# A given order of products for the merging projections of a two-branch encoder layer, with source tiles loaded one at a time

## The chip, the cores and the metric

The kernel runs on one core of a Trainium2 chip. The core has five engines with a queue of instructions each: TensorE (PE, matrix products, with its weight loads shown apart as PEld), VectorE (DVE), ScalarE (ACT), GpSimd (POOL) and SyncE (SP, which here only issues DMAs). Each engine runs its own queue in order, and semaphores make it wait for the others. DMAs are issued from the queues of SP, ACT and POOL. Operands lie in an on-chip memory of 128 partitions (SBUF); matrix products are summed up in banks of 128 x 512 numbers (PSUM). The metric is the device time of one execution in microseconds (us); of several runs the median counts.

## What is computed

One encoder layer is applied to two groups of 512 tokens with the same weights, in float32. What matters here is the middle of the layer, where two branches are projected to the model's width, merged by gates, and projected once more:

```python
y_m = (jax.nn.sigmoid(o) * hm.astype(x.dtype)) @ w_mo      # branch (A), mLSTM
...
y_a = mla_attention(q_nope, q_rope, k_nope, k_rope, va) @ w_ao   # branch (B), attention
g_m, g_a = jnp.split(jax.nn.sigmoid(gm), 2, axis=-1)
x = x + (g_m * y_m + g_a * y_a) @ w_out
```

Both `w_mo` and `w_ao` are 1024 x 1024. The feed-forward network, a gated embedding and a last norm follow.

## The kernel before, in words

**Exact products out of rounded ones.** PE multiplies a rounded float32 type. Each operand is therefore cut into a rounded part (hi: a cast on ACT) and the rest (lo: a subtraction on DVE, `lo_of`, L168), and each product is made of three matmuls: hi x hi, hi x lo, lo x hi. In `product` these are the lines L857, L858 and L859; for four slices of 128 rows a product has 12 matmuls of 128 x 512.

**Seven products in place of eight.** The class `Seven` multiplies a pair of column blocks (c and c + 4) of a weight with both token groups at once. With two blocks of weights and two groups there would be eight half-length products; it makes seven, named P1, P2, P7, P6, P5, Q4 and P3, from sums of the weight's four quarters a11, a12 (the first source tile of 512 KB) and a21, a22 (the second). `source` makes these sums in place: for P7 s = a11 + a21 (L818) and a21 += a22 (L819), for P6 a11 += a21 (L821), for P3 a12 += a11 (L828). They run on POOL, but for three pairs on DVE (the first and the last of `w_mo`, the first of `w_ao`). The other factor's sums and cuts are made by `Ops.part` and `Ops.need` (L748 to L770). The products of a pair are summed up in three banks: b1 takes P1, then P6, P5 and P3, and between them ACT copies it (L911); b0 takes P2; b2 takes P7, then Q4. DVE combines them (L916), and `put_z` or `put_y` multiplies with the gate and adds (L1239, L1520, L1521).

**The stage.** There are eight pairs: 0 to 3 for `w_mo` (operands `hops`), 4 to 7 for `w_ao` (operands `oops`, the attention's output). P1, P2, P7 and P6 of pair 0 run inside the last units of the attention, whose instructions keep an order written out by hand (`pinned`). In the loop over units, u is the unit, and the slots named "a", "mid", "d", "late" and so on hold extra work for it; `pairs[i].ahead` cuts a weight early there. The 52 other products run in `chain(quads, made=pairs, ...)` (the call follows L1530). Its order before, with the pair's number ahead of the product's name:

```
1P1 1P2 1P7 0P5 0Q4 0P3 | 1P6 2P1 1P5 2P2 1Q4 2P7 1P3 | 2P6 3P1 2P5 3P2 2Q4 3P7 2P3
3P6 4P1 3P5 4P2 3Q4 4P7 3P3 | 4P6 5P1 4P5 5P2 4Q4 5P7 4P3 | 5P6 6P1 5P5 6P2 5Q4 5P3
6P6 6P7 6P5 7P1 6Q4 6P3 | 7P6 7P7 7P5 7P2 7Q4 7P3
```

This is the order in which the instructions are traced. A planner with a simulated timeline then orders each engine's queue from it, and it may move instructions past each other, unless they are told to keep the program's order (`pinned`, or for matmuls `mmpin`) or to be issued behind another instruction of the same engine (`issue_after`).

**Buffers.** Cut weights have five buffers in turn (`wpair`), hi and lo of a product side by side, so a weight can be cut when the product five before it has been done. Source tiles: `wring` gives a pair's first tile one of three buffers in turn (two in pool WP, one in OP), the second tile one of two (pool WX). A pair's first tile is read until P3's cut, its second until Q4's. Both are loaded in the constructor of `Seven` (`S.dma_start`, L804), that is from ACT's queue, when `chain` makes the pair, one product ahead of its first use. The operands P1, P2, P7 and P6 lie in 32 buffers of pool H, and those of `oops` take over those of `hops`; P5, Q4 and P3 lie in 24 buffers of pool OP. `chain` asks for operands four products ahead (`look`).

**After the stage.** The merged values are cut (L1541, L1543) and go into `out_proj` (L197 to L199); later the feed-forward network runs through `chain` again, with `head=True`.

Of the kernel before, what the change touches and what calls it, by code (L numbers as in the profile page):

```python
# [62 lines left out]
def encoder_kernel(ctx: ExitStack, tc: tile.TileContext, a):  # L63
# [3 lines left out]
    class Engine:  # L67


        def __init__(self, e):  # L70
            self.e = e
# [133 lines left out]
    def rsqrt(src, n, scale):  # L205
# [22 lines left out]
        return y2  # L228

# [545 lines left out]
    wpn, wsn = [0], [0]  # L775
# [12 lines left out]
    def wsplit(src):  # L788
        n, t = src.shape[-1], wpair()
        hi, lo = t[:, 0:n], t[:, n : 2 * n]  # L790
        S.copy(hi, src)  # L791
        lo_of(lo, src, hi)
        return hi, lo

    class Seven:


        def __init__(self, srcs, kh, ops, out, adds=None):
            n = kh * P
            self.adds = adds or GP  # L800
            st = []
            for sl, src in zip(wring(wsn[0]), srcs):
                t = sl("wst", "wst", F32, (P, 1024))
                S.dma_start(t[:, : 2 * n], src)  # L804
                st += [t[:, 0:n], t[:, n : 2 * n]]
            wsn[0] += 1
            self.st, self.n, self.kh, self.ops, self.out = st, n, kh, ops, out
            self.bk, self.w = {}, {}

        def source(self, name):  # L810
            n, (a11, a12, a21, a22) = self.n, self.st
# [18 lines left out]
            return src  # L830

# [31 lines left out]
    def chain(quads, head=False, look=4, made=(), done=(), two=False, hook=None):  # L863

        order = [(0, n) for n in ("P1", "P2", "P7")]
# [22 lines left out]
        order = [o for o in order if o not in done]  # L888
# [5 lines left out]
        for at, (q, n) in enumerate(order):  # L894
            for i, m in order[at : at + look + 1]:
                quads[i][0].need(m)
            for i, _ in order[at : at + 2]:
                make(i)
            mmpin[0] = head and q == len(quads) - 1
            made[q].product(n)  # L900
            mmpin[0] = False
            if hook and (q, n) in hook:
                hook[q, n]()
# [340 lines left out]
    def pair(kind, c, ops, put):  # L1244
        e = V if (kind, c) in (("mo", 0), ("mo", 3), ("ao", 0)) else GP
        srcs = [a["w8"][W8[f"{kind}{i}"]] for i in (c, c + 4)]
        return ops, lambda: Seven(srcs, 4, ops, outputs(put), e)
# [55 lines left out]
    for u in range(NU + 1):  # L1303
# [83 lines left out]
        if u == 14:  # L1387
            todo_ = {"mid": [(ahead_hi, "P2")], "d": [(ahead_lo, "P2")], "late": [(ahead_hi, "P7")], "f": [(ahead_lo, "P7")]}
        pre = lambda name, out=True: pairs[0].product(name, out)
# [138 lines left out]
    with ExitStack() as behind:  # L1528
# [4 lines left out]
        chain(quads, made=pairs, done=[(0, n) for n in ("P1", "P2", "P7", "P6")])  # L1533
# [205 lines left out]
    chain(quads, head=True)  # L1739
# [162 lines left out]

LEAD = 2
# [98 lines left out]
```

## Time and profile before

| | us |
|---|---|
| three timed runs | 1850.92, 1852.28, 1853.04 |
| their median | 1852.28 |
| the profiled execution | 1848.15 |
| its span, from the first to the last instruction | 1846.4 |

The profile is of one execution. It gives the busy time of each engine and a chain of work that ended last. A row of the timeline has a start in us from the span's start, a length in us, the engine, the line of the kernel (L79 stands for all instructions with a pinned order), the operation, the tiles as out<-in, shapes, and in brackets the engine's idle time before it with what ended that. Matmuls are pipelined: each is shown with its full length of about 0.39 us, though the next starts earlier, so the time from start to start says more than the length. ACTq, SPq are the queues' issuing of DMAs, which does not count as busy. The granted clock of PE was 0.997 of full speed over the span.

### The profile page before, as it was taken

What the parts mean: (1) busy time and instruction counts of PE and PEld (TensorE: products, weight loads), DVE (VectorE), ACT (ScalarE), POOL (GpSimd) and SP (SyncE); (2) the same over time, 40 slices, a digit from 0 to 9 for tenths busy, and PEclk for the clock granted to TensorE, in tenths of its full rate; (3) what the DMA queues carried; (4) which work ended last, traced back from release to release, by engine and by line L of the source; (5) the groups of instructions that cost most, each with busy time, mean ns of one, the idle gap of its engine ahead of it and who ended that gap; (6) DMA issues with size and microseconds to landing.
All of it is one profiled execution on the core that took longest, in us unless ns stands there. A gap on an engine that the chain in (4) does not pass through costs nothing.

```text
span 1846.4 us, 24616 instructions
## 1 busy us (share of the span) xinstructions
PE 1817.5 (98%) x8767; PEld 1512.0 (82%) x8767; DVE 1281.5 (69%) x2154; ACT 892.1 (48%) x1752; POOL 429.8 (23%) x353
## 2 busy tenths in 40 slices
PE   9999999999999999999999999999999999999997
PEld 7889898988887888877877888888888887888786
DVE  6767576857667787778887586444444569978756
ACT  6256556563454566664543364333333344434433
POOL 0101010200032222213420005664566523111000
PEclk9999999999999999999999999999999999999998
DMA  4211112123353443267555331322223246533332
GB/s 168 67 58 52 63 52 71 45 75 126 126 172 128 149 137 115 81 211 239 183 177 185 113 141 69 126 92 97 97 91 131 97 157 237 161 133 100 103 141 99
DMA packets 104619, 224.65 MB, mean 122 GB/s; under 512 B 12856, under 2 KB 23536, under 8 KB 104496
## 3 DMA queue, kind: packets, MB, share of 16 engines
q1 hardware_dynamic: 85440, 158.02, 25.6%
q10 hardware_dynamic: 13248, 47.19, 7.6%
q0 software_dynamic: 5808, 17.86, 3.0%
q8 instruction: 69, 1.13, 0.3%
q14 instruction: 54, 0.44, 0.1%
HBM read 164.57 MB, written 54.26 MB: 119 GB/s over the span
## 4 chain that ended last, share of the span: by engine, by line
PE 85%; DVE 9%; ACT 2%; DMA 2%; issue 1%; POOL 0%; SPq 0%; DVEq 0%; ACTq 0%
PE b L857 13%; PE b L859 13%; PE b L858 12%; PE mm L197 6%; PE mm L199 6%; PE mm L198 6%; PE sc L79 4%; PE mm L79 3%; PE nm L643 3%; PE l L79 3%; PE av L79 2%; PE pt L79 1%; PE mm L563 1%; DVE xl L168 1%; PE mm L562 1%; PE mm L561 1%
## 5 line engine op out<-in xcount | busy, mean ns | idle before, releaser
L857 PE MATMUL b<-xh,wp 128*128 128x512 f32 x1051 | 403.8, 392 | 7.0 <-ACT wp L791 4.3
L858 PE MATMUL b<-xl,wp 128*128 128x512 f32 x1051 | 409.5, 391 | 0.7 <-DVE xl L168 0.7
L859 PE MATMUL b<-xh,wp 128*128 128x512 f32 x1051 | 406.9, 391 | 2.0 <-DVE wp L168 2.0
L791 ACT CAST wp<-wst 128x512 fp32r<-128x512 f32 (+1 forms) x289 | 176.2, 613 | 304.2 <-PE b L859 247.0
L168 DVE TENSOR_TENSOR wp<-wst,wp 128x512 fp32r<-128x512 f32 (+1 forms) x289 | 246.4, 855 | 73.8 <-ACT wp L791 68.9
L857 PEld LDWEIGHTS b<-xh,wp 128*128 128x128 f32 x1051 | 197.3, 188 | 55.2 <-ACT u L911 6.3
L859 PEld LDWEIGHTS b<-xh,wp 128*128 128x128 f32 x1051 | 197.3, 188 | 45.8 <-DVE wp L168 2.8
L858 PEld LDWEIGHTS b<-xl,wp 128*128 128x128 f32 x1051 | 197.3, 188 | 43.6 <-DVE xl L168 1.1
L197 PE MATMUL mm<-hh,whi 128*128 128x512 f32 x432 | 169.2, 392 | 0.1
L198 PE MATMUL mm<-hl,whi 128*128 128x512 f32 x432 | 168.8, 391 | 0.0
L199 PE MATMUL mm<-hh,wlo 128*128 128x512 f32 x432 | 168.2, 391 | 0.0
L916 DVE TENSOR_TENSOR u<-b,u 128x512 f32<-128x512 f32 x95 | 65.3, 688 | 139.0 <-PE b L859 80.5
L818 POOL TENSOR_TENSOR s<-wst,wst 128x512 f32<-128x512 f32 (+1 forms) x33 | 56.2, 1702 | 333.0 <-DMA wst<-w 163.2
L1661 POOL TENSOR_TENSOR sg<-sg,u 128x512 f32<-128x512 f32 x30 | 55.0, 1833 | 202.6 <-DVE u L916 202.6
L911 ACT COPY u<-b 128x512 f32<-128x512 f32 x93 | 52.6, 588 | 94.9 <-PE b L859 67.6
L199 PEld LDWEIGHTS mm<-hh,wlo 128*128 128x128 f32 x432 | 81.1, 188 | 16.9
L197 PEld LDWEIGHTS mm<-hh,whi 128*128 128x128 f32 x432 | 81.1, 188 | 16.7 <-ACT raw L79 0.5
L198 PEld LDWEIGHTS mm<-hl,whi 128*128 128x128 f32 x432 | 81.1, 188 | 16.6
L182 ACT CAST whi<-wst 128x1024 fp32r<-128x1024 f32 x53 | 55.6, 1049 | 73.9 <-PE mm L198 36.4
L168 DVE TENSOR_TENSOR xl<-ld,xh 128x512 fp32r<-128x512 f32 x105 | 84.3, 830 | 0.6 <-ACT xh L1692 0.5
L609 POOL TENSOR_TENSOR b<-b,mask 128x512 f32<-128x512 f32 x16 | 24.5, 1536 | 228.4 <-DMA b<-nmd 169.4
L168 DVE TENSOR_TENSOR wlo<-wst,whi 128x1024 fp32r<-128x1024 f32 (+2 forms) x56 | 67.1, 1199 | 12.1 <-ACT whi L182 11.7
(446 smaller groups left out, 4034.5 us busy)
## 6 DMA issues: line engine op xcount, KB each, us to landing
wst<-w ACTq DMA_DIRECT2D x68, 512.0 KB
wst<-w SPq DMA_DIRECT2D x65, 512.0 KB
ld<-actd SPq DMA_DIRECT2D x77, 256.0 KB
actd<-t SPq DMA_DIRECT2D x40, 256.0 KB
x<-x SPq DMA_DIRECT2D x32, 256.0 KB
wst<-wd ACTq DMA_DIRECT2D x16, 512.0 KB
actd<-sg SPq DMA_DIRECT2D x30, 256.0 KB
ld<-hzd SPq DMA_DIRECT2D x28, 256.0 KB
```

The lines of the kernel that those rows point to most:

```text
L79: r = f(*args, **kw)
L168: e.tensor_tensor(out=out, in0=src, in1=hi.bitcast(F32), op=ALU.subtract)
L182: S.copy(hi[:, :n], st[:, :n])
L197: E.matmul(bk, whi[:, c], hi, start=k == 0, stop=False)
L198: E.matmul(bk, whi[:, c], lo, start=False, stop=False)
L199: last_mm[0] = E.matmul(bk, wlo[:, c], hi, start=False, stop=k == nk - 1)
L791: S.copy(hi, src)
L818: self.adds.tensor_tensor(out=src, in0=a11, in1=a21, op=ALU.add)
L857: E.matmul(bk, whi[:, c], hi, start=bool(first) and k == 0, stop=False, **sk)
L858: E.matmul(bk, whi[:, c], lo, start=False, stop=False, **sk)
L859: E.matmul(bk, wlo[:, c], hi, start=False, stop=k == self.kh - 1, **sk)
L916: V.tensor_tensor(out=t, in0=b, in1=t, op=ALU.add if name == "P2" else ALU.subtract)
```

## The change

Five things change.

- `chain` can be given an order, and the merging projections get one, `MERGE`. Up to the product 1Q4 it is the order from before; then the pairs 2 and 3 alternate product by product, and after them 4 and 5; 6 and 7 follow as before. The matmuls of pair 7 keep their program order, with 7P2 and 7Q4 between 7P5 and 7P3.
- `Seven` can be made without its loads (`parts=True`, for all pairs but 0 and 1), and `fetch` loads one source tile. In `MERGE`, `2w` behind a product fetches the next tile of pair 2; the load is issued on ACT behind the latest cast of a weight (`cast[0]`).
- The two sums for P7 of pair 1 are made by POOL in the attention's unit 14, the last but one, in slot "a" (`summed`), and `source` later returns the ready tile.
- In the chain of the feed-forward network the loads of the first pairs are issued behind the last weight cast of the merging projections (`after=merged`).
- A tile of 32 bytes a partition, `pad`, is allocated in the pool `sm` and never used.

```diff
+    sm.tile([P, 8], F32, name="pad", tag="pad", bufs=1)
...
-    wpn, wsn = [0], [0]
+    wpn, wsn, cast = [0], [0], [None]
...
-        S.copy(hi, src)
+        cast[0] = S.copy(hi, src).ins
         lo_of(lo, src, hi)
...
-        def __init__(self, srcs, kh, ops, out, adds=None):
+        def __init__(self, srcs, kh, ops, out, adds=None, parts=False):
             n = kh * P
             self.adds = adds or GP
-            st = []
-            for sl, src in zip(wring(wsn[0]), srcs):
-                t = sl("wst", "wst", F32, (P, 1024))
-                S.dma_start(t[:, : 2 * n], src)
-                st += [t[:, 0:n], t[:, n : 2 * n]]
+            self.st, self.n, self.kh, self.ops, self.out = [], n, kh, ops, out
+            self.todo = list(zip(wring(wsn[0]), srcs))
             wsn[0] += 1
-            self.st, self.n, self.kh, self.ops, self.out = st, n, kh, ops, out
-            self.bk, self.w = {}, {}
+            while self.todo and not parts:
+                self.fetch()
+            self.bk, self.w, self.made = {}, {}, {}
+
+        def fetch(self):
+            sl, src = self.todo.pop(0)
+            t = sl("wst", "wst", F32, (P, 1024))
+            S.dma_start(t[:, : 2 * self.n], src)
+            self.st += [t[:, 0 : self.n], t[:, self.n : 2 * self.n]]

         def source(self, name):
-            n, (a11, a12, a21, a22) = self.n, self.st
+            if name in self.made:
+                return self.made[name]
+            n, (a11, a12, a21, a22) = self.n, (self.st + [None] * 2)[:4]
...
+        def summed(self, name, e):
+            e, self.adds = self.adds, e
+            self.made[name] = self.source(name)
+            self.adds = e
...
-    def chain(quads, head=False, look=4, made=(), done=(), two=False, hook=None):
+    def chain(quads, head=False, look=4, made=(), done=(), two=False, hook=None, order=None, after=None):
...
-        order = [o for o in order if o not in done]
+        if given:
+            order = [(int(o[0]), o[1:]) for o in given if o[1] != "w"]
+            fetch = {}
+            for o in given:
+                if o[1] == "w":
+                    fetch.setdefault(at, []).append(int(o[0]))
+                else:
+                    at = int(o[0]), o[1:]
+        else:
+            order = [o for o in order if o not in done]
...
             for i, _ in order[at : at + 2]:
-                make(i)
-            mmpin[0] = head and q == len(quads) - 1
+                with tc.issue_after(after) if after and at < 4 else nullcontext():
+                    make(i)
+            mmpin[0] = (head or given) and q >= len(quads) - (1 if head else 1)
             made[q].product(n)
             mmpin[0] = False
+            for i in fetch.get((q, n), ()) if given else ():
+                with tc.issue_after(cast[0]):
+                    make(i)
+                    made[i].fetch()
...
-        return ops, lambda: Seven(srcs, 4, ops, outputs(put), e)
+        return ops, lambda: Seven(srcs, 4, ops, outputs(put), e, c > 1 or kind == "ao")
...
             todo_ = {"mid": [(ahead_hi, "P2")], "d": [(ahead_lo, "P2")], "late": [(ahead_hi, "P7")], "f": [(ahead_lo, "P7")]}
+            todo_["a"] = todo_.get("a", []) + [(lambda: pairs[1].summed("P7", GP),)]
...
-        chain(quads, made=pairs, done=[(0, n) for n in ("P1", "P2", "P7", "P6")])
+        chain(quads, made=pairs, order=MERGE.split())
+        merged = cast[0]
...
-    chain(quads, head=True)
+    chain(quads, head=True, after=merged)
...
+MERGE = """
+1P1 2w 1P2 1P7 0P5 0Q4 2w 0P3 3w 1P6 2P1 1P5 2P2 1Q4 3P1 3w 1P3 3P2 4w
+2P7 3P7 2P6 3P6 2P5 3P5 2Q4 4P1 4w 2P3 4P2 5w 3Q4 5P1 5w 3P3 5P2 6w
+4P7 5P7 4P6 5P6 4P5 5P5 4Q4 6P1 6w 4P3 6P2 7w 5Q4 5P3 7w
+6P6 6P7 6P5 7P1 6Q4 6P3 7P6 7P7 7P5 7P2 7Q4 7P3
+"""
```

More of the change, by code (lines that the diff above doesn't have):

```diff
@@ L1 @@
-from contextlib import ExitStack
+from contextlib import ExitStack, nullcontext
 import concourse.bass as bass
@@ L861, in product @@
                 self.out(name, self.bk)
-    def chain(quads, head=False, look=4, made=(), done=(), two=False, hook=None):
-        order = [(0, n) for n in ("P1", "P2", "P7")]
+    def chain(quads, head=False, look=4, made=(), done=(), two=False, hook=None, order=None, after=None):
+        given, order = order, [(0, n) for n in ("P1", "P2", "P7")]
         if head:
```

## The prediction

> **What bounds the kernel now.** I read the page first, for the engine that sets the end.
>
> ```profile
> span 1846.4 us, 24616 instructions
> ...
> PE 1817.5 (98%) x8767; PEld 1512.0 (82%) x8767; DVE 1281.5 (69%) x2154; ACT 892.1 (48%) x1752; POOL 429.8 (23%) x353
> ...
> PE 85%; DVE 9%; ACT 2%; DMA 2%; issue 1%; POOL 0%; SPq 0%; DVEq 0%; ACTq 0%
> ```
>
> TensorE is busy for 98% of the span and holds 85% of the chain that ended last. The change removes no matmul, so all that it can give is idle time of PE. I therefore went to the busy time by stretch, for the 52 products that the chain of merging projections still has to run when it starts at 836 us. Columns: stretch, its length, busy us (and count) of PE, weight loads, DVE, ACT, POOL, then granted clock, DMA share, GB/s.
>
> ```profile
> 836.00:852.00 16.00, 12.39 (x53) 9.26 (x51) 14.18 (x18) 11.57 (x23) 12.87 (x7) 1.00 0.71 233
> 852.00:922.00 70.00, 70.00 (x306) 57.37 (x307) 60.98 (x96) 31.19 (x56) 21.96 (x6) 1.00 0.61 200
> 922.00:930.00 8.00, 5.56 (x24) 3.88 (x23) 8.00 (x13) 5.25 (x11) 0.50 (x1) 1.00 0.86 247
> 930.00:950.00 20.00, 20.00 (x89) 16.43 (x88) 19.50 (x26) 6.93 (x13) 6.16 (x4) 1.00 0.61 191
> 950.00:988.00 38.00, 36.65 (x159) 29.51 (x158) 32.70 (x50) 17.65 (x30) 5.81 (x4) 1.00 0.59 198
> 836.00:988.00 152.00, 144.60 (x625) 116.44 (x624) 135.37 (x200) 72.59 (x129) 47.30 (x21) 1.00 0.63 204
> ```
>
> The second row has no idle PE: 70.00 / 306 = 0.2288 us a matmul, so a product of 12 takes 2.745 us. 52 products need 142.8 us; the stage takes 152.0. **The most that this stage can give is 9.2 us**, 0.5% of the kernel. By the rows PE idles 152.00 - 144.60 = 7.40 us; the other 1.8 us are restarts. The timeline shows where (start, length, engine, line, operation, idle time before and what ended it):
>
> ```profile
> 837.98 4.63 POOL L818 TENSOR_TENSOR s<-wst,wst 128x512 f32<-128x512 f32 x1
> 842.64 0.62 ACT L791 CAST wp<-s 128x512 fp32r<-128x512 f32 x1 [3.07 <-POOL s L818]
> 843.31 0.50 PE L857 MATMUL b<-xh,wp 128*128 128x512 f32 x1 [1.25 <-ACT wp L791]
> 844.44 1.78 DVE L168 TENSOR_TENSOR xl<-ld,xh 128x512 fp32r<-128x512 f32 x1
> 849.55 0.68 DVE L916 TENSOR_TENSOR u<-b,u 128x512 f32<-128x512 f32 x1
> 849.68 0.50 PE L858 MATMUL l<-xl,wp 128*128 128x512 f32 x1 [0.80 <-DVE xl L168]
> 851.97 0.50 PE L859 MATMUL b<-xh,wp 128*128 128x512 f32 x1 [1.56 <-DVE wp L168]
> ...
> 903.04 7.04 POOL L818 TENSOR_TENSOR s<-wst,wst 128x512 f32<-128x512 f32 x1 [41.62 <-DMA wst<-w]
> 910.15 8.94 POOL L819 TENSOR_TENSOR wst<-wst 128x512 f32<-128x512 f32 x1
> 919.17 1.63 POOL L821 TENSOR_TENSOR wst<-wst,wst 128x512 f32<-128x512 f32 x1
> 919.57 1.78 DVE L168 TENSOR_TENSOR wp<-wst,wp 128x512 fp32r<-128x512 f32 x1
> 923.68 0.62 ACT L770 CAST xh<-t 128x512 fp32r<-128x512 f32 x1 [3.23 <-DVE t L757]
> 924.21 0.61 ACT L791 CAST wp<-s 128x512 fp32r<-128x512 f32 x1
> 924.88 0.50 PE L857 MATMUL b<-xh,wp 128*128 128x512 f32 x1 [1.69 <-ACT wp L791]
> 928.50 0.34 ACTq L804 DMA_DIRECT2D wst<-w  x1
> 928.90 0.62 ACT L791 CAST wp<-wst 128x512 fp32r<-128x512 f32 x1
> 929.57 0.50 PE L857 MATMUL b<-xh,wp 128*128 128x512 f32 x1 [0.74 <-ACT wp L791]
> ...
> 951.54 0.50 PE L857 MATMUL b<-xh,wp 128*128 128x512 f32 x1 [0.68 <-ACT u L911]
> 982.69 0.50 PE L857 MATMUL b<-xh,wp 128*128 128x512 f32 x1 [0.68 <-ACT u L911]
> ```
>
> Seven stalls: 1.25 + 0.80 + 1.56 + 1.69 + 0.74 + 0.68 + 0.68 = 7.40 us, the whole idle time; 1.8 / 7 = 0.26 us a restart. Three causes. At the start, POOL's sum for pair 1's P7 takes 4.63 us, the cast waits 3.07 us for it, and POOL's further sums then make DVE's subtractions 1.78 us long, where the addition that reads a PSUM bank (849.55) takes 0.68 amid them. In the middle DVE has no idle time (8.00 of 8.00 us): the attention operands are being cut, POOL's sums for pair 5 lie among them, ACT stands behind a cast that waits for DVE, and the weight cast stands behind that. The two of 0.68 us are a product that adds to a bank which ACT is still copying.
>
> **The change, part by part.** I number the 52 products in program order from 0, so product n starts at 836.2 + 2.745 n us if nothing stalls.
>
> *The sum made early.* Pair 1's two sums for P7 (L818, L819) move from 838 us into the attention unit before the last. Gone at the start are the wait of 1.25 us and two of POOL's seven operations there. What is late next is DVE: of the shown stretch it is busy 14.18 of 16 us, and the last operand of product 5 (0P3) needs 12 operand subtractions, 6 weight subtractions and 2 evacuations after 838.99 us. At 60.98 / 96 = 0.635 us that is 12.7 us, done at 851.7; PE wants it, at its fourth slice of product 5, at 836.2 + 5 x 2.745 + 9 x 0.229 = 852.0. So it just fits if POOL keeps away. But pair 1's other two sums and one or two of pair 2's still fall there, each worth 1.78 - 0.69 = 1.09 us on DVE: 3.3 us late with three. The three stalls cost 3.61 + 3 x 0.26 = 4.39 us; the bounds of the saving are 1.1 and 4.39, and I take 2.7, the middle.
>
> What the moved sums do in the attention stage has these rows:
>
> ```profile
> 802.64 0.57 POOL L79 DMA_DIRECT2D ozd<-oz  x1 [3.56 <-DVE oz L79]
> 805.75 0.69 DVE L79 TENSOR_TENSOR ql<-l,qh 128x512 fp32r<-128x512 f32 x1 [1.75 <-ACT qh L79]
> 807.12 0.52 POOL L79 DMA_DIRECT2D rsd<-rb  x1 [3.91 <-ACT rb L79]
> 809.83 1.95 DVE L79 TENSOR_TENSOR s<-wst,wst 128x512 f32<-128x512 f32 x1
> 813.76 0.49 PE L79 MATMUL sc<-qh,ql 128*128 128x512 f32 x1 [1.37 <-DVE ql L79]
> ```
>
> POOL is free from 803.2 to 807.1 us and DVE has a hole of 1.75 us before 805.75, so two sums of 1.6 us nearly fit; the store of the row sums behind them on POOL may wait a little. But one DVE operation can be caught, and one unit later just that (the 1.95 us sum, then a late ql) cost PE 1.37 us. Bounds 0 and 1.37 + 0.26 = 1.63; I take 0.7 us lost, the near half.
>
> *The alternating order.* Until product 10 the order is the same. Then 3P1, 3P2, 3P7 and 3P6 run at 11, 13, 15, 17 instead of 14, 16, 18, 20, which frees the operand buffers that the attention operands are cut into 3 products earlier. 4P1 and 4P2 stay at 21 and 23, while 4P7, 4P6, 4P5 and 4Q4 move from 25, 27, 29, 31 to 28, 30, 32, 34. DVE gets 3 to 6 products (8 to 16 us) more for the same 44 operations. Counted from product 11 to 34, DVE has about 96 operations: 61 us at 0.635, against 23 x 2.745 = 63 us of PE. Five POOL sums at 1.09 us, if they take turns with DVE, turn the 2 us of slack into 3 us of lateness. So the middle's 2.43 + 2 x 0.26 = 2.95 us may go or come back whole: bounds 0 and 2.95 saved, I take 1.6. The alternation puts another pair's product between 4P6 and 4P5 and between 5P6 and 5P5, 2.745 us for a copy of 0.59; that is the stall at 951.54, 0.94 us with its restart, of which I take 0.5, since only the last pair's matmuls are held in order and the planner may still pull equal pairs together.
>
> *The last pair held in order.* 7P2 and 7Q4 then stand between 7P5 and 7P3, 5.5 us for the same copy: the stall at 982.69 goes, 0.94 us. The product that out_proj's first group needs, 7Q4, is now last but one, so the next stage starts no later.
>
> *Tiles fetched singly behind casts.* No transfer is added; each 512 KB load is issued from ACT right after a cast instead of where the planner puts it. Before, an issue can block ACT while its buffer is read (928.50 lies between two casts). Lead times stay ample:
>
> ```profile
> 898.11 0.33 ACTq L804 DMA_DIRECT2D wst<-w  x1
> ...
> L791 ACT CAST wp<-wst 128x512 fp32r<-128x512 f32 x43 | 26.4, 623 | 37.0 <-PE b L859 26.6 <-PE l L859 5.1 <-DVE wp L168 4.0
> ```
>
> From the issue at 898.11 to the sum that it releases at 903.04 pass 4.93 us. The casts wait for PE most of all (26.6 of 37.0 us), so they run as far ahead as five weight buffers allow, and a load behind a cast is about five products early. The first loads of the next chain go behind the last cast; they are due over 100 us later. The saving is inside the 1.6 above. Zero beside it.
>
> *Padding.* It moves the buffers allocated after it by 32 bytes. No row compares two placements. Both kinds of weight buffer that the chain alternates have the same rows, and PE's pitch is 0.2288 us throughout, so zero; either sign of 1 us stays in the range.
>
> Sum: 2.7 + 1.6 + 0.5 + 0.94 - 0.7 = 5.0 us. The profiled execution took 1848.15 us (1.75 around its span), so 1843.1; it was 4.13 us under the median 1852.28 of the timed runs, and carried to the median the forecast is **1847.3 us**.
>
> **The rivals.** *All goes* (saves 7 to 9.2 us, 1844 us): DVE's work fits. For it, DVE's 135.37 busy us contain the POOL delays, and 200 x 0.635 = 127 us fit in 142.8. Against it, the work comes in lumps (8.00 of 8.00 us).
>
> *DVE sets the pace anyway* (saves 1.7 us, 1850.6): the stalls shrink at the start, return between 30 and 36, and the attention unit pays 1.6. This includes that the change does not do what it says, because only pair 7 is held and the planner orders the rest: before, it already mixed l and b matmuls from 841 to 850 us. For it, the count of 61 against 63 us.
>
> *Starved sums* (slower): pair 6's second tile is now fetched behind 6P1's cast (product 35) instead of behind 4Q4 at 31, and three POOL sums must follow before 6P6 at 40. The cast of 6P7 waits for them, and on ACT the copies and casts of the following products stand behind it. With casts five products ahead there are 9 x 2.745 = 24.7 us, less 4.93 for the load and 2.6 for two casts and subtractions: 17.2 us. Undisturbed the sums take 5; starved as at 903 they take 7.04 + 8.94 + 1.63 = 17.6. It decides from there: if casts run only two products ahead, 8.9 us are left, PE stalls 8.7 us, and with the start's 2.7 gained the kernel takes 1852.3 + 6.0 = 1858.3. Against it stands the casts' waiting for PE. The Trainium skill (SBUF — State Buffer, Who interferes with whom) says that a VectorE instruction with two SBUF inputs and a GpSimd one that reads SBUF exclude each other for a whole instruction, whichever starts first. The trace agrees on who collides (1.78 us against 0.68 for the one that reads PSUM), but a wait for one instruction would make a sum some 2.0 us, three of them 6, and this rival would be worth nothing; the 8.94 us row says that a dense DVE gets in again and again, so I keep it.
>
> **How the numbers follow.** A measurement of this kernel can tell about 0.2%, 3.7 us, from no change (the three runs lie within 2.1 us). Forecast, 3.7 to 7 us saved (1845.3 to 1848.6): 0.42. All goes (1843.1 to 1845.3): 0.13. DVE's pace (1848.6 to 1856.0): 0.29. Starved sums: 0.16. So faster 0.55, same 0.29, slower 0.16. The range goes from 1843.0, the floor, to 1854.5; beyond lie the starved sums and the edge of DVE's pace, under 2 in 10. The faster cases alone span 1843.0 to 1848.6.
>
> **What would show it.** Right: no POOL sum between 837 and 841, PE's idle before the third product gone, PE idle in the chain at 3 to 4 us instead of 7.40, and the stage near 146 us. Alternation shows as products in l and b turning about 15 to 20. Wrong: an idle PE ended by the cast of s between 6P1 and 6P6, POOL rows of 7 us there, a PE wait for ql near 806 us longer than 1.4 us, or new stalls after the stage, which I expect unchanged.

## The result and the profile after

| | runs | median, us | range, us |
|---|---|---|---|
| before, on the same chip | 5 | 1851.25 | 1849.84 to 1853.04 |
| after | 5 | 1841.14 | 1839.54 to 1842.20 |

The ratio is 0.9942, with a 95% interval of 0.9929 to 0.9956: the change saves some 10 us where 5 were forecast, and 1841.14 lies below the range's low end of 1843.0. The profiled execution took 1841.67 us.

The page of the changed kernel, for the engine that sets the end:

```profile
span 1839.9 us, 24627 instructions
...
PE 1813.5 (99%) x8767; PEld 1514.4 (82%) x8767; DVE 1281.0 (70%) x2154; ACT 891.6 (48%) x1752; POOL 422.5 (23%) x353
...
PE 81%; DVE 11%; DMA 3%; ACT 2%; issue 2%; POOL 0%; SPq 0%; DVEq 0%; ACTq 0%
```

PE runs the same 8767 matmuls and is still the bound, but it is busy for 1813.5 us in place of 1817.5. The forecast had only idle time go, so a busy time that falls by 4 us already says that something else happened. It falls although this profile has 6.8 us near 410 us in which PE was granted half its clock (shown in the last section). By the starts of the matmuls that cost 3.3 us, and the profile of before has nothing like it: without it the two profiles would differ by 9.8 us, not by 6.5.

The busy time by stretch of the merging projections, from their first matmul to the first of `out_proj` (columns as in the prediction: stretch, length, busy us and count of PE, weight loads, DVE, ACT, POOL, clock, DMA share, GB/s):

```profile
838.95:854.95 16.00, 14.78 (x64) 11.55 (x62) 15.87 (x21) 13.14 (x25) 12.61 (x5) 1.00 0.83 280
854.95:926.95 72.00, 71.62 (x316) 59.28 (x317) 64.98 (x98) 32.52 (x57) 9.95 (x6) 1.00 0.60 190
926.95:934.95 8.00, 7.08 (x32) 5.51 (x31) 8.00 (x14) 5.92 (x11) 0.00 (x0) 1.00 0.95 310
934.95:983.89 48.94, 48.94 (x218) 40.52 (x216) 46.34 (x66) 19.66 (x34) 13.87 (x8) 1.00 0.60 199
838.95:983.89 144.94, 142.42 (x626) 116.87 (x624) 135.19 (x196) 71.23 (x127) 36.43 (x19) 1.00 0.64 209
```

The stage takes 144.94 us, where it took 152.0, and PE idles 144.94 - 142.42 = 2.52 us in it in place of 7.40. In its last 48.94 us PE has no idle time at all.

The timeline of the same kernel shows the sums, what is late now, and what follows the stage:

```profile
805.94 1.31 POOL L79 TENSOR_TENSOR s<-wst,wst 128x512 f32<-128x512 f32 x1
807.33 1.30 POOL L79 TENSOR_TENSOR wst<-wst 128x512 f32<-128x512 f32 x1
...
816.50 0.49 PE L79 MATMUL sc<-qh,ql 128*128 128x512 f32 x1 [1.39 <-DVE ql L79]
...
840.70 7.11 POOL L829 TENSOR_TENSOR wst<-wst,wst 128x512 f32<-128x512 f32 x1
847.89 1.63 POOL L836 TENSOR_TENSOR wst<-wst 128x512 f32<-128x512 f32 x1
849.48 1.73 POOL L826 TENSOR_TENSOR s<-wst,wst 128x512 f32<-128x512 f32 x1
849.99 3.48 DVE L168 TENSOR_TENSOR xl<-ld,xh 128x512 fp32r<-128x512 f32 x2
851.29 1.63 POOL L827 TENSOR_TENSOR wst<-wst 128x512 f32<-128x512 f32 x1
...
855.33 0.50 PE L872 MATMUL b<-xh,wp 128*128 128x512 f32 x1 [1.49 <-DVE wp L168]
...
904.98 1.89 POOL L826 TENSOR_TENSOR s<-wst,wst 128x512 f32<-128x512 f32 x1 [42.65 <-DMA wst<-w]
906.94 1.62 POOL L827 TENSOR_TENSOR wst<-wst 128x512 f32<-128x512 f32 x1
...
929.34 0.50 PE L870 MATMUL b<-xh,wp 128*128 128x512 f32 x1 [0.92 <-ACT u L938]
...
936.94 1.99 POOL L826 TENSOR_TENSOR s<-wst,wst 128x512 f32<-128x512 f32 x1 [24.99 <-DMA wst<-w]
...
986.90 0.50 PE L197 MATMUL mm<-yh,whi 128*128 128x512 f32 x1 [0.36 <-ACT yh L1570]
996.35 0.50 PE L197 MATMUL mm<-yh,whi 128*128 128x512 f32 x1 [0.50 <-ACT whi L182]
997.30 0.50 PE L197 MATMUL mm<-yh,whi 128*128 128x512 f32 x1 [0.22 <-ACT whi L182]
```

(L826, L827, L829 and L836 are the lines L818, L819, L821 and L828 of before, L938 the copy L911, L870 to L872 the matmuls.) The two early sums take 1.3 us each, and the wait for ql behind them is no longer than before (1.39 and 1.37 us). The sums of pair 5, which took 7.04 and 8.94 us before, take 1.89 and 1.62. Two stalls of some size are left in the stage (1.49 and 0.92 us), and `out_proj` has new small ones.

Put together from the starts of the matmuls, which count a stall with its restart: the stage gains 7.1 us, of which 5.95 are stalls (9.28 to 3.33) and 1.1 the pitch, the time from one matmul's start to the next's (228.8 to 226.9 ns). From `out_proj`'s first matmul to the feed-forward network's chain 1.3 us are given back (113.62 to 114.92), and the 2772 matmuls of that chain take 636.89 us, not 639.77. So the gain has two parts: stalls in the stage, and a shorter pitch everywhere, which no step of the forecast holds.

### The profile page after: what moved, and what is told of

Same layout as the page of the kernel before. It is cut to its first block, busy times and chain, and to the rows that moved or that the text cites. A ratio compares the mean times of both kernels' runs of the same rounds, so it can differ in the third digit from the quotient of the medians.

```text
span 1839.9 us, 24627 instructions
## 1 busy us (share of the span) xinstructions
PE 1813.5 (99%) x8767; PEld 1514.4 (82%) x8767; DVE 1281.0 (70%) x2154; ACT 891.6 (48%) x1752; POOL 422.5 (23%) x353
## 4 chain that ended last, share of the span: by engine, by line
PE 81%; DVE 11%; DMA 3%; ACT 2%; issue 2%; POOL 0%; SPq 0%; DVEq 0%; ACTq 0%
PE b L870 11%; PE b L872 11%; PE b L871 11%; PE mm L197 6%; PE mm L199 6%; PE mm L198 6%; PE sc L79 4%; PE mm L79 3%; PE nm L645 3%; PE l L79 3%; PE av L79 2%; DVE xl L168 2%; DVE wp L168 2%; PE pt L79 2%; PE mm L565 1%
## 5 line engine op out<-in xcount | busy, mean ns | idle before, releaser
L871 PE MATMUL b<-xl,wp 128*128 128x512 f32 x1023 | 397.2, 389 | 0.8 <-DVE xl L168 0.8
L872 PE MATMUL b<-xh,wp 128*128 128x512 f32 x1023 | 393.9, 390 | 2.4 <-DVE wp L168 2.4
L870 PE MATMUL b<-xh,wp 128*128 128x512 f32 x1023 | 391.0, 390 | 3.7 <-ACT u L938 2.3
L793 ACT CAST wp<-wst 128x512 fp32r<-128x512 f32 (+1 forms) x289 | 176.4, 613 | 293.9 <-PE b L872 227.8
L870 PEld LDWEIGHTS b<-xh,wp 128*128 128x128 f32 x1023 | 192.0, 188 | 48.0 <-ACT u L938 5.2
L872 PEld LDWEIGHTS b<-xh,wp 128*128 128x128 f32 x1023 | 192.0, 188 | 43.9 <-DVE wp L168 3.9
L871 PEld LDWEIGHTS b<-xl,wp 128*128 128x128 f32 x1023 | 192.0, 188 | 40.8 <-DVE xl L168 1.2
L826 POOL TENSOR_TENSOR s<-wst,wst 128x512 f32<-128x512 f32 (+1 forms) x32 | 46.8, 1462 | 342.3 <-DMA wst<-w 145.1
L938 ACT COPY u<-b 128x512 f32<-128x512 f32 x93 | 52.5, 588 | 89.0 <-PE b L872 60.2
L168 DVE TENSOR_TENSOR wlo<-wst,whi 128x1024 fp32r<-128x1024 f32 (+2 forms) x56 | 67.1, 1200 | 11.6 <-ACT whi L182 11.2
```

The costliest lines, as they stand in the source:

```text
L168: e.tensor_tensor(out=out, in0=src, in1=hi.bitcast(F32), op=ALU.subtract)
L793: cast[0] = S.copy(hi, src).ins
L870: E.matmul(bk, whi[:, c], hi, start=bool(first) and k == 0, stop=False, **sk)
L871: E.matmul(bk, whi[:, c], lo, start=False, stop=False, **sk)
L872: E.matmul(bk, wlo[:, c], hi, start=False, stop=k == self.kh - 1, **sk)
```

## Experiments: the padding

The first question was which part of the change moves what. Two kernels split off the padding: the kernel before with the padding alone, and the changed kernel without it. Each engine's instructions stand in the same order as in the kernel that it comes from.

```diff
 (pad_alone: the kernel before)
+    sm.tile([P, 8], F32, name="pad", tag="pad", bufs=1)
 (after_no_pad: the changed kernel)
-    sm.tile([P, 8], F32, name="pad", tag="pad", bufs=1)
```

> The kernel before with the unused 32-byte tile and nothing else; every engine's instructions stand in the same order as before, only buffers lie 32 bytes further. Theory A (placement sets PE's pitch): in the chain of 836 to 988 us the matmuls go from 0.2288 to about 0.227 us, in the feed-forward chain from 0.2285 to 0.227; 624 x 1.9 ns + 2709 x 1.7 ns = 5.8 us, less 0 to 2 us of stalls that a faster PE meets, so 4 to 6 us faster than before (1845 to 1847 us). The stalls of the stage stay at about 7.4 us. Theory B (the order and its traffic set the pitch, the padding does nothing): no change, 1851 us, pitch 0.2288.

> The changed kernel without the unused tile; every engine's instructions stand in the same order as in the changed kernel. Theory A: pitch back at 0.2285 to 0.2288 us in both chains, 4 to 6 us slower than the changed kernel, so 1845 to 1847 us, 0.2 to 0.3% faster than the kernel before; the stage still idles some 3 us in place of 7.4. Theory B: 1841 us and a pitch of 0.227.

Measured: pad_alone 1847.52 us beside 1852.04 of the kernel before, ratio 0.9974 (0.9964 to 0.9983); after_no_pad 1847.43 us, 0.9977 (0.9966 to 0.9987). **The padding alone saves 4.5 us, the other four changes together 4.6**, and the product of the two ratios, 0.9951, agrees with 0.9942 within the intervals.

A tile that nothing reads can only act by the addresses of what is allocated behind it. The same 503 matmuls of the feed-forward network's chain, none of which waits, stand in one row for each kernel (the view by stretch); first before, then after, pad_alone and after_no_pad:

```profile
1293.42:1408.06 114.64, 114.64 (x503) 94.24 (x502) 53.91 (x63) 40.38 (x72) 68.44 (x45) 1.00 0.29 101
```

```profile
1289.07:1402.91 113.84, 113.84 (x503) 94.22 (x502) 53.29 (x63) 40.35 (x72) 69.01 (x45) 1.00 0.30 103
```

```profile
1293.64:1407.47 113.83, 113.83 (x503) 94.22 (x502) 52.98 (x63) 40.50 (x72) 69.35 (x45) 1.00 0.30 102
```

```profile
1289.88:1404.52 114.64, 114.64 (x503) 94.23 (x502) 53.93 (x63) 40.36 (x72) 68.25 (x45) 1.00 0.29 101
```

114.64 us without the padding, 113.84 with it, whatever the order; the clock is 1.00 and the other engines do the same. PE counts as busy throughout, which is why a view of idle time can't show it. Where it comes from is seen when the starts of the matmuls are taken in groups of twelve, as many as a product has (us, from the twelfth matmul of this stretch on; the planner mixes products, so a group can hold parts of two):

```
before  2.794 2.724 2.720 2.720 2.728 2.795 2.724 2.728 2.793 2.765 2.720 2.720
after   2.719 2.721 2.720 2.720 2.720 2.720 2.720 2.720 2.720 2.720 2.720 2.720
```

Before, some groups take about 2.79 us and most 2.72; after, all take 2.72. Of the five buffers for cut weights in turn, four lie in pool WP at the low addresses of SBUF (its left) and one in pool WX at the high ones (its right). The compiled programs give the address of every buffer within a partition, so each matmul of the profile can be put beside the address of its moving operand (nearly all in pools H and OP; the attention's pools Q and QL are left out) and of the weights that are loaded during it, for the matmul after it. Mean time from start to start, of the matmuls of 512 columns in the rounded type that follow at once, by the difference of the two addresses (weights less moving operand, modulo 128 bytes):

| kernel | H, OP / WP / WX, address modulo 128 | difference 0, ns (count) | other differences |
|---|---|---|---|
| before | 64 / 64 / 96 | 227.6 ns (4848) | 32: 233.0 (793); 64: 229.2 (79) |
| after | 96 / 96 / 96 | 227.2 (5544) | 64: 229.5 (83) |

The pad moves the left side by 32 bytes and the right side stays, so all three come to stand alike. 793 matmuls (898 with those that the table leaves out, since a wait follows or the shape is another) by 5.4 to 5.7 ns are 4.3 to 5.1 us, the 4.5 that were measured. Two smaller terms partly cancel beside it. Matmul for matmul, with half clock left out, the profile of pad_alone has the slow ones 5.2 us shorter than before, those with difference 0 another 2.0 us (0.35 ns each; why is open), and the stalls 2.9 us longer, together 4.2 us.

Two more kernels tested this by moving buffers the other way. minus_32 takes 32 bytes away ahead of the pools, by putting two constants of one column into one tile, so that left and right differ by 64. pad_behind_weights puts the 32 bytes between the weights' pool WP and all else, so that H, OP and WX agree, but the four weight buffers of WP differ from them.

```diff
 (minus_32: the kernel before)
-    one = cp.tile([P, 1], F32, name="one")
+    two_ = cp.tile([P, 2], F32, name="one")
+    one = two_[:, 0:1]
...
-    first = cp.tile([P, 1], F32, name="first")
+    first = two_[:, 1:2]
 (pad_behind_weights: the kernel before)
     WP = Slots("WP", wst=2, whi=2, wlo=2)
+    PD = Slots("PD", pd=1)
+    PD("pd", "pd", F32, (P, 8))
     EV = Slots("EV", ch=2, bk=2)
...
+    PD.close()
```

> The kernel before with two one-column constants put in one tile, so that every buffer allocated after them lies 32 bytes lower instead of higher; the order of instructions is as before. Moving operands and the weight buffers of pool WP then lie at 32, those of WX at 96, modulo 128. In the profile of the kernel before, a matmul during which weights are loaded that lie 32 bytes off the moving operand modulo 128 takes 233.0 ns from start to start, one without that offset 227.3 ns. Theory A1 (only the offset modulo 64 counts): the difference is now 64, no matmul is slow, pitch 0.227 us, 4 to 6 us faster than before, like the padding alone. Theory A2 (the two must agree modulo 128): the 865 matmuls stay slow and the time is that of before within 1.5 us.

> The kernel before with the unused 32 bytes allocated behind pool WP, so that moving operands lie at 96 with WX, and the weights in WP stay at 64, modulo 128; the order of instructions is as before. 5401 matmuls in place of 898 then load weights 32 bytes off. Theory A (the offset costs 5.7 ns, in either direction): (5401 + 905 - 898) x 5.7 ns = 31 us slower than before, about 1882 us, nearly all of it in the projections, whose pitch goes from 0.2272 to 0.233. Theory A' (only weights above the operand cost): no change. Theory C (where a buffer lies in itself counts, 64 is bad and 96 is good): faster by the operands' share, 2 to 5 us.

Measured: minus_32 1852.39 us beside 1852.47, ratio 1.0 (0.999 to 1.0009); pad_behind_weights 1871.42 us, 1.0102 (1.0088 to 1.0116), 19 us slower. The same 503 matmuls, first in minus_32, then in pad_behind_weights:

```profile
1295.14:1409.94 114.80, 114.80 (x503) 94.26 (x502) 52.87 (x63) 40.34 (x72) 68.56 (x45) 1.00 0.30 101
```

```profile
1309.75:1426.32 116.57, 116.57 (x503) 94.12 (x502) 52.42 (x63) 40.36 (x72) 68.23 (x45) 1.00 0.29 100
```

| kernel | H, OP / WP / WX, address modulo 128 | difference 0 | other differences |
|---|---|---|---|
| minus_32 | 32 / 32 / 96 | 227.8 ns (4841) | 64: 232.3 (872) |
| pad_behind_weights | 96 / 64 / 96 | 228.5 (876) | 96: 233.3 (4667); 32: 233.3 (120) |

In pad_behind_weights the roles are exchanged: WX, slow before, is the fast one (228.2 ns beside H), and WP, fast before, is slow (233.3). (The 120 with a difference of 32 have their moving operand in pools WP and M1.) So neither pool nor its place counts, only whether the two addresses agree. A difference of 64 bytes costs about as much as one of 32 or 96. The size was 19 us where the expectation gave 31. Its sum adds 905 matmuls that it does not explain; (5401 - 898) x 5.7 ns are 25.7 us. Matmul for matmul against before, the matmuls with weights from WP are 28.7 us longer and those from WX 4.0 shorter, so 24.7 as counted; the stalls are 5.0 us shorter, since a slower PE waits less for others, matmuls of other shapes 1.5 shorter, and the rest 0.9 longer. That makes 19.1 us, as measured; the profiles differ by 4.7 us more, the cost of 10.2 us at half clock.

## Experiments: the order, the sums, the loads

The remaining 4.6 us were split by undoing one part of the changed kernel at a time. Stage is the time from the first matmul of the merging projections to the first of `out_proj`; stalls are gaps between starts above the pitch, with restarts.

| kernel | ratio to before (95%) | median / before, us | stage, us | stalls, us |
|---|---|---|---|---|
| before | | | 152.04 | 9.28 |
| after | 0.9942 (0.9929 to 0.9956) | 1841.14 / 1851.25 | 144.95 | 3.33 |
| after_no_pad | 0.9977 (0.9966 to 0.9987) | 1847.43 / 1852.04 | 145.60 | 3.00 |
| pad_alone | 0.9974 (0.9964 to 0.9983) | 1847.52 / 1852.04 | 153.05 | 11.2 |
| pad_sum_old_order | 0.9953 (0.9939 to 0.9966) | 1843.14 / 1852.04 | 150.95 | 9.16 |
| after_no_early_sum | 0.9954 (0.9941 to 0.9966) | 1843.85 / 1852.04 | 147.69 | 5.99 |
| after_both_tiles | 0.9945 (0.9931 to 0.9958) | 1843.67 / 1852.47 | 145.81 | 4.18 |
| after_no_pin | 0.9944 (0.9931 to 0.9957) | 1842.20 / 1852.47 | 149.00 | 7.30 |
| after_loads_free | 0.9960 (0.9949 to 0.9972) | 1844.29 / 1851.83 | 147.71 | 6.01 |
| after_four_pinned | 0.9970 (0.9958 to 0.9982) | 1846.18 / 1851.83 | 150.80 | 9.01 |
| after_all_sums_early | 0.9927 (0.9915 to 0.9939) | 1838.59 / 1851.83 | 143.26 | 1.71 |

The intervals are about 2.5 us to either side, so ratios that differ by under 0.002 are hardly told apart. The stage and its stalls come from one execution each. In pad_alone, pad_sum_old_order and after_four_pinned, 3.4 us at half clock fall into the stage; some 1.4 to 1.6 us of their stage and of their stalls are that. Apart from it, kernels with the same order of instructions agree within 0.5 us of stalls (before 9.3, minus_32 9.4, pad_alone 9.7; after 3.3, after_no_pad 3.0), so differences of 1 us and more are read from these columns.

**Without the early sum.**

```diff
-            todo_["a"] = todo_.get("a", []) + [(lambda: pairs[1].summed("P7", GP),)]
```

> The changed kernel with pair 1's two sums for P7 made where they were before, when P7 is due. Theory: the three stalls at the start come back from 1.9 to about 4.1 us, so 2 us slower than the changed kernel (1843 us), and the attention's unit before the last is unchanged. Rival: the alternating order leaves PE enough other work at the start, and the time stays within 0.5 us of 1841.

```profile
840.68 4.69 POOL L826 TENSOR_TENSOR s<-wst,wst 128x512 f32<-128x512 f32 x1
...
846.07 0.50 PE L870 MATMUL b<-xh,wp 128*128 128x512 f32 x1 [1.32 <-ACT wp L793]
...
852.43 0.50 PE L871 MATMUL l<-xl,wp 128*128 128x512 f32 x1 [0.81 <-DVE xl L168]
...
854.72 0.50 PE L872 MATMUL b<-xh,wp 128*128 128x512 f32 x1 [1.56 <-DVE wp L168]
```

In the timeline the three stalls of before are back in their old sizes (1.32, 0.81, 1.56 us against 1.25, 0.80, 1.56), and the stage is 2.7 us longer. So the early sum is worth 2.7 us of stalls; by the ratio 2.2, which alone would not be told from nothing.

**The old order, with padding and early sum kept.**

```diff
-        return ops, lambda: Seven(srcs, 4, ops, outputs(put), e, c > 1 or kind == "ao")
+        return ops, lambda: Seven(srcs, 4, ops, outputs(put), e)
...
-        chain(quads, made=pairs, order=MERGE.split())
+        chain(quads, made=pairs, done=[(0, n) for n in ("P1", "P2", "P7", "P6")])
...
-    chain(quads, head=True, after=merged)
+    chain(quads, head=True)
```

> The changed kernel with the old order of products: the padding and the early sums for pair 1 stay; the given order, the single loads, the order of the last pair and the loads behind the last cast go. If the early sums alone mend the start (4.4 us of stalls become about 2) and the alternation mends the middle and the two copies' stalls (4.8 us), this kernel keeps the stalls near 922, 928, 951 and 982 us and takes 1841 + 3 to 5 = 1844 to 1846 us. Rival: DVE is late whatever the order is, and the stalls of the middle vanish because the whole stage is earlier relative to POOL; then it stays within 1 us of 1841.

```profile
906.80 8.94 POOL L827 TENSOR_TENSOR wst<-wst 128x512 f32<-128x512 f32 x1
...
920.32 0.62 ACT L772 CAST xh<-t 128x512 fp32r<-128x512 f32 x1 [3.90 <-DVE t L759]
920.85 0.61 ACT L793 CAST wp<-s 128x512 fp32r<-128x512 f32 x1
...
921.51 0.79 PE L870 MATMUL b<-xh,wp 128*128 128x512 f32 x1 [2.41 <-ACT wp L793]
```

Without the half clock the stage is some 4.6 us longer than with the given order. By the ratio the kernel loses 2.0 us, less than the 3 to 5 expected, and the intervals overlap. Pair 5's second sum takes 8.94 us again, as it did before; with the given order it takes 1.62 us. The stall of 2.41 us is not a wait for that sum, which ended at 915.74. The weight's cast stands on ACT behind an operand's cast, and that one waited 3.90 us for DVE. What the given order changes is how far DVE is ahead. The operands first used between 904 and 920 us were cut 5 us earlier on average in before and here (at least 2.9 and 2.4 us), and 16 us earlier in the changed kernel (at least 11.1). The single loads, the pin or the held loads undone alone (the next runs) leave it at 15 to 16 us, so the order itself is what does it. Why a sum is long or short has another reason, shown in the last section.

**Both source tiles at once**, in place of one behind each cast; and **the last pair not held in order**.

```diff
 (after_both_tiles)
-                    made[i].fetch()
+                    if made[i].todo:
+                        made[i].fetch()
...
-        return ops, lambda: Seven(srcs, 4, ops, outputs(put), e, c > 1 or kind == "ao")
+        return ops, lambda: Seven(srcs, 4, ops, outputs(put), e)
 (after_no_pin)
-            mmpin[0] = (head or given) and q >= len(quads) - (1 if head else 1)
+            mmpin[0] = head and q == len(quads) - 1
```

> The changed kernel with both source tiles of a pair loaded when the pair is made, at the first of its two fetches, instead of one at a time. The second tile's buffer is then often still read, so the load's issue stands in ACT's queue ahead of casts and copies. If the single loads matter: 1 to 5 us slower than the changed kernel (1842 to 1846 us), with PE stalls ended by casts or copies between 870 and 945 us. If they do not (my prediction priced them at zero): within 0.7 us.

> The changed kernel with the matmuls of pair 7 left to the planner. If it then puts 7P3 right behind 7P5 as before, the stall of 0.68 us near 982 us (0.9 with its restart) comes back and the kernel is 0.5 to 1 us slower than the changed one; but the 1.3 us that the next stage now stalls more than before (2.6 in place of 1.25 us by starts) may go with it, and then the time stays within 0.7 us of 1841.

The stall that each brings, in its timeline; first after_both_tiles, then after_no_pin:

```profile
869.71 0.50 PE L872 MATMUL l<-xh,wp 128*128 128x512 f32 x1 [0.49 <-DVE wp L168]
```

```profile
979.08 0.50 PE L870 MATMUL b<-xh,wp 128*128 128x512 f32 x1 [2.03 <-ACT u L938]
982.53 0.50 PE L870 MATMUL b<-xh,wp 128*128 128x512 f32 x1 [0.44 <-DVE u L943]
```

The single loads are worth one stall of 0.5 us (0.8 with its restart), which the ratio (0.9945) can't tell from nothing. Without the pin the planner puts products of pair 7 side by side, and PE waits 2.03 us for the copy of their bank; the stage loses 4.05 us. But the stretch after it is 1.43 us shorter (113.49 against 114.92), in it `out_proj` has none of the three stalls shown above, and the time is the same (0.9944). So about a third of the pin's gain is given back in the next stage; the other 2.6 us lie within the spread of the ratios, and the time doesn't show them.

**The next chain's first loads where the planner puts them.**

```diff
-    chain(quads, head=True, after=merged)
+    chain(quads, head=True)
```

> The changed kernel without the wait of the next chain's first loads for the last weight cast of the merging projections; the planner places them where it likes. Theory (that step is worth nothing): the ratio stays at 0.9942 within 0.0008, the stage at 145 us. Rival: the loads are issued from ACT inside the stage, an issue blocks ACT while its buffer is still read, and the casts behind it come late: one or two stalls of 0.6 to 0.9 us more, 0.9946 to 0.9952.

The forecast had named this step and put it at nothing; the rival was right here, and the loss (0.9960) is larger than the one that it named. ACT and PE in its timeline:

```profile
950.69 0.62 ACT L793 CAST wp<-wst 128x512 fp32r<-128x512 f32 x1 [3.00 <-PE b L872]
...
956.02 0.34 ACTq L813 DMA_DIRECT2D wst<-w  x1
956.39 0.58 ACT L938 COPY u<-l 128x512 f32<-128x512 f32 x1 [5.08 <-DVE wp L168]
...
957.03 0.50 PE L870 MATMUL l<-xh,wp 128*128 128x512 f32 x1 [1.85 <-ACT u L938]
```

A load for the next chain stands on ACT's queue at 951.3 and waits until DVE has read its buffer; the copy behind it is held for 5.08 us, and PE for 1.85. The stage is 2.8 us longer, the ratio 0.0018 larger. That a load which nobody needs for 100 us can stop PE is a matter of the queue that it stands in, not of the transfer.

**More held in order; more sums made early.** The last two looked for a better version. One holds pairs 4 to 7 in program order, the other makes pair 1's remaining two sums on POOL at the end of the attention's last unit.

```diff
 (after_four_pinned)
-            mmpin[0] = (head or given) and q >= len(quads) - (1 if head else 1)
+            mmpin[0] = head and q == len(quads) - 1 or bool(given) and q >= 4
 (after_all_sums_early, at the end of the last unit)
+            pairs[1].summed("P6", GP)
+            pairs[1].summed("P3", GP)
```

> The changed kernel, with the matmuls of pairs 4 to 7 held in program order instead of those of pair 7 alone. Theory: the stall of 1.08 us at 927.8 is a copy of a bank that the next product adds to; the planner has pulled two products of one pair side by side. Held in the given order, another pair's product lies between, the stall goes, and the stage takes 143.9 us instead of 144.95; ratio 0.9936. Rival: the stall is late work of ACT behind DVE, which the planner's order hides in part; held in order, PE waits for operands or casts instead, the stalls of the stage grow past 4 us, and the ratio is 0.995 or more.

> The changed kernel, with pair 1's last two sums (for P6 and for P3) also made on POOL inside the attention, at the end of its last unit, instead of in the stage. Theory: of the stalls that are left at the start of the merge stage, 0.28 us before the second product and 1.65 us at 853.2 come from DVE, which is slowed by POOL's sums at 847.9 to 853. With two sums fewer there, the stalls at the start fall from 1.9 us to 0.3 or less, the stage from 144.95 to 143.2 us, and the ratio to the kernel before goes from 0.9942 to about 0.9933, 1839.5 us. Rival: DVE has its full count of cuts there in any case, 12.7 us of work for 15 us, so the stalls stay at 1.9 us and the time at 0.9942; if the two sums get in the way of the last cuts of the attention, it is 1 to 2 us slower, 0.995.

Timeline of after_four_pinned:

```profile
923.44 0.51 PE L79 MATMUL b<-xl,wp 128*128 128x512 f32 x1 [0.99 <-DVE xl L168]
...
925.85 0.79 PE L79 MATMUL b<-xl,wp 128*128 128x512 f32 x1 [1.43 <-DVE xl L168]
```

The rival was right: held in order, PE waits for the operand cuts of DVE, which the planner's order had covered with other products' matmuls; the stalls grow to 9.01 us, or some 7.7 without the half clock. So the planner's shuffling in the middle is worth more than the one copy stall that it makes (0.92 us at 929.34).

Timeline of after_all_sums_early, and below it its stage in the view by stretch:

```profile
834.96 1.28 POOL L79 TENSOR_TENSOR wst<-wst,wst 128x512 f32<-128x512 f32 x1 [2.67 <-DVE wp L79]
836.94 1.29 POOL L79 TENSOR_TENSOR wst<-wst 128x512 f32<-128x512 f32 x1 [0.69 <-DVE wp L79]
...
927.85 0.50 PE L870 MATMUL b<-xh,wp 128*128 128x512 f32 x1 [0.98 <-ACT u L938]
```

```profile
839.13:982.39 143.26, 142.08 (x626) 117.00 (x624) 134.28 (x199) 70.91 (x127) 33.01 (x17) 1.00 0.65 211
```

The sums take 1.3 us in the attention, where one of them took 7.11 us in the stage and both lay among DVE's cuts; the stalls of the stage's first 80 us are gone, and it takes 143.26 us, as expected. The time, 1838.59 us or 0.9927, is the lowest of all; against the changed kernel's 0.9942 the intervals overlap, so the gain rests on the stage's own rows (1.7 us) more than on the ratio.

## Why the prediction was right in sign and wrong in size

- **What bounds the kernel**: right as far as it went. The stage's idle PE was the place of half the gain. But "all that it can give is idle time of PE" was false: the same matmuls got shorter.
- **Padding**: the step that failed. The forecast put it at zero because "No row compares two placements" and because both kinds of weight buffer "have the same rows, and PE's pitch is 0.2288 us throughout". It saves 4.5 us. The 0.2288 was a mean of two pitches, 0.2276 for four of five weight buffers and 0.2330 for the fifth: 0.2276 + 0.2 x 0.0054 = 0.2287. The two placements stood in the trace of before, product by product; they were never taken apart by buffer. The bound of 1 us to either side was therefore wrong too, and with it the floor of 1843.0.
- **The sum made early**: 2.7 us forecast, 2.7 of stalls measured (2.2 by the ratio). Two of its three stalls went, and of DVE's lateness 1.49 us stayed, for the reason given: POOL's other sums of pair 1 still fall there (7.11, 1.63 us). after_all_sums_early shows that these were the cause.
- **Its cost in the attention**: 0.7 us forecast, nothing measured. POOL had the hole that the forecast found (805.94 to 808.63), and the wait for ql that was feared is 1.39 us as it was before, 1.37. The stage begins at 838.94 us with the early sum and at 838.93 without it, with 6.8 us at half clock ahead of it in both.
- **The alternating order, with the loads**: 1.6 us for the middle and 0.5 for the copy. Before, the middle's two stalls near 925 and the one at 951 took 1.69 + 0.74 + 0.68 = 3.11 us of idle; after, 0.92 is left of them: 2.2 us gone beside the 2.1. The reason given, time for DVE, holds: the operands are cut 16 us ahead of their first use in place of 5. That pair 5's sums are no longer starved as well (1.62 against 8.94 us) was not forecast.
- **The last pair held in order**: the stall of 0.68 us at 982.69 is gone, as forecast. That "the next stage starts no later" holds too, but "new stalls after the stage, which I expect unchanged" does not: it gives back 1.3 us. Without the pin, in the new order, more would have been lost than 0.94 (4.05 us in the stage).
- **Tiles fetched behind casts**: zero forecast. Right for the single tiles; wrong for the loads of the next chain: holding them back saves 2.8 us of the stage in the new order.
- **The sum**: the four parts other than padding were forecast at 5.0 us and measured at 4.6 by medians (ratio 0.9977, 2.4 to 6.3 us). That part of the working carried, in part by luck: by the ratios, undoing the order with its loads and pin costs 2.0 us, undoing the held loads alone 3.3 (forecast at nothing) and the pin alone 0.4 (forecast at 0.94), so its terms are not each confirmed.
- **The rivals**: *DVE sets the pace* is out, with 2.52 us of idle time left of 7.40. *Starved sums* did not occur: pair 6's first sum begins at 936.94 and takes 1.99 us, no 17.6 for three. The rule of the Trainium skill (SBUF — State Buffer, Who interferes with whom) that was weighed there is that one of the two engines excludes the other for a whole instruction. Read as a wait of one instruction, so some 2 us a sum, it fits these rows, while the 7.11 us at 840.70 again does not. What the forecast took from the 8.94 us, that a dense DVE gets in again and again, holds until DVE reads from PSUM or falls idle (last section). *All goes* came nearest in time, for a reason that it did not hold.

## What to carry to other kernels

A mean pitch is a number to take apart: group the starts of matmuls by the buffers that they read before calling it a property of the engine. Where operands and weights come from pools on both sides of the memory, compare their addresses modulo 128 bytes; a few bytes of padding can be worth as much as a reordering. Before a load is issued early, see what stands behind it on its queue; and a sum on a slow engine costs least where the fast engine has holes or reads from PSUM, not where its result is wanted.

## What the runs showed of the hardware

**Weights and moving operand in step.** A matmul of 512 columns with its moving operand in pool H or OP, during which the next weights are loaded, takes 227 to 228.5 ns from start to start if both addresses agree modulo 128 bytes, and 232 to 233 ns if they differ by 32, 64 or 96 (some 790 to 4700 matmuls each, in four kernels; two groups of about 80 with a difference of 64 lie at 229 ns). Which weights count, those being loaded or the matmul's own, shows where a row of matmuls changes its weight buffer. With 64, in minus_32, 160 matmuls whose own weights agree and only the next differ take 227.0 ns, and 95 the other way round 230.7; most of the two groups at 229 ns are of the first kind. With 32, in before, both kinds are slow (105 at 234.8 and 96 at 232.2 ns). This is not all that sets the pitch: in the attention (pools Q and QL) some 640 matmuls of before whose addresses agree take 230 to 232 ns. Differences of multiples of 512 bytes are free (some 540 to 830 matmuls at each, in the changed kernel, all at 227 ns); 128, 256 and 384 did not occur, so the period may be any of 128, 256 and 512. What in the memory or in PE makes it so, no run shows.

**A sum on POOL beside a dense DVE.** Thirty of the stage's sums on POOL, in the 13 profiles, take longer than 2.3 us (2.35 to 8.94). Each ends 1.1 to 1.3 us after DVE has either begun an instruction that reads a PSUM bank or fallen idle. DVE's rows for three of them and for a short one, of 1.89 us; first two of before, then two of after:

```profile
908.83 0.69 DVE L916 TENSOR_TENSOR u<-b,u 128x512 f32<-128x512 f32 x1
917.85 0.69 DVE L1239 SCALAR_TENSOR_TENSOR ld<-ld,l 128x512 f32<-128x512 f32 x1
```

```profile
846.58 0.68 DVE L943 TENSOR_TENSOR u<-b,u 128x512 f32<-128x512 f32 x1
905.62 0.68 DVE L1266 SCALAR_TENSOR_TENSOR ld<-ld,b 128x512 f32<-128x512 f32 x1
```

The sums end at 910.08, 919.10, 847.81 and 906.87. Until then DVE's instructions with both inputs in SBUF follow each other at 0.6 us and the sum gets nowhere; then it is done in the 1.2 us, and mostly the two engines take turns from there, with sums of 1.62 us and DVE's instructions at 1.78. DVE has no idle time in either case (16.13 of 16.13 us beside pair 5's first two sums in before, 6.97 of 6.97 beside its four in after). So it is not a less busy DVE that made pair 5's sums short, but a PSUM read 0.6 us behind their start, where before it came 5.8 us later. Why the turns, once taken, sometimes end again (the sum at 910.15) no run shows.

**Half clock for some microseconds.** In most profiles PE's granted clock falls to half for 3.4 or 6.8 us, near 10 or 410 us or behind stalls in the stage. The view by stretch of before and then of after, at the same place in the program's course:

```profile
408.00:416.00 8.00, 8.00 (x50) 7.12 (x50) 3.74 (x8) 6.21 (x16) 2.77 (x4) 1.00 0.21 71
```

```profile
408.00:416.00 8.00, 8.00 (x36) 7.04 (x36) 3.48 (x7) 5.82 (x15) 3.15 (x5) 0.62 0.29 83
```

The mean clock is 0.62 (0.50 from 410 to 416 us), and 36 matmuls run in the time of 50. PE was not idle ahead of it (busy for 20.00 of 20.00 us from 390 on). Of the 13 profiles here only two, before and after_no_pin, have no such event ahead of the last 30 us. It costs about half its length, 1.7 to 3.4 us, as much as an edit of this change, so profiles were compared by stage and not by their ends. Why one execution has it and another not was not settled.
